# Modulation columns all on VectorE, two branches pulled forward, and the later modulation sums tied to stages of the delta rule

## The chip, the cores and the metric

The kernel runs on one core of one Trainium2 chip. The metric is the device time of one execution in microseconds (us). TensorE (PE) multiplies matrices, VectorE (DVE) does elementwise arithmetic and reductions, ScalarE (ACT) evaluates functions and copies, GpSimd (POOL) fills and issues a few transfers, and SyncE (SP) issues nearly all the transfers from HBM.

## The reference, cut to what the change touches

The model has a mixing block with four branches and a feed-forward part, and then two attention layers. Only the mixing block is touched. Its input has 512 tokens of 1024 features:

```
c_act = silu(c)
sh1, sc1, gt1, sh2, sc2, gt2 = split(c_act @ ada_w + ada_b, 6)     # 48 columns of 128 values
h = rms_norm(x, norm_mix_g) * (1 + sc1) + sh1
p = h @ w_in
y_a = rwkv7 delta rule (token shift, low-rank decays, two groups of two heads, chunks of 64)
y_b = gelu(p_u) * (causal w_s @ layer_norm(gelu(p_v)))             # gated branch
y_c = short convolution of width 3
y_d = s5: complex diagonal state space, then gelu and a gated product
x = x + gt1 * ((sum of sigmoid(gates) * y) @ w_o)
```

## The kernel before, in words

Every product is kept near full precision by splitting both operands into a high and a low part: a weight slab is loaded into `raw` (a ring of four buffers), ScalarE writes `whi`, VectorE writes `wlo` (three buffers each, lines 150 to 163), and `mm3` (line 178) makes three TensorE products for each pair of 128-row pieces. A slab of 128 output columns is thus 24 products of 512 columns.

The code is traced in program order, and a list scheduler then orders each engine's instructions by when it thinks that they are ready, earlier traced work first among what is ready. Buffers are asked for in the same way. `tc.issue_after(i)` adds an edge of order alone: what is traced in the block on the engine of `i` is queued behind `i`.

`_start` (line 374) makes the columns 8 to 15 of the modulation (sc1), two at a time. Six of them are dot products on VectorE (`tensor_tensor_reduce`, 1024 elements in each partition). Columns 8 and 15 (`BY_PE`) are made on TensorE from another layout of the weights, `ada_k`, and from the column form of c, `c_col`. Each pair of columns gives `g1` (line 444), which scales the x tiles (lines 448 to 455); the first three projection slabs run as the pairs come.

`_first_block` (line 1252) then runs the other four slabs of the delta rule's projection with the shift columns 0 to 7, small tables of the state space (`_s5_setup`), the convolution (`_conv_branch`, six slabs), and the gated branch (`_sg_branch`): four value products `svp` (96 matmuls), gelu and layer norm on VectorE, then two gate slabs and the small mixing matmuls `sgm`. `_merge(K, 2, ...)` sums the convolution with its gates: eight slabs, each of nine pieces (24 `gp` products, 6 `yp` products). At its piece 26 the large state space tables are traced (`_s5_tables`). After it come `_rwkv_shift` and all of `_s5_branch`: two projection slabs, transposes (`s5b`, `s5c`), input products `s5w`, a chain on VectorE with two scans that ends in the tiles `xb` (line 1216), then the output products `s5y` (line 1225) and more transposes.

Last come the two head groups of the delta rule, `_wkv`, a generator of 50 stages each. Stages 13 to 27 are five levels of three stages (`pu`, `pmt`, `pm`), 33 to 39 carry the state (`st`), and 40 to 47 make the output. Pieces of the merges 1 and 3 are poured between the stages as fill: 42 pieces first, then 1.3 for each stage. From stage 18 of either group every second stage also asks for one of the modulation columns 16 to 47: its weights go into the ring `raw`, and VectorE makes the dot product (`_dot`, line 333).

Of the kernel before, what the change touches and what calls it, by code (L numbers as in the profile page):

```python
# [17 lines left out]
AF = mybir.ActivationFunctionType  # L18
OP = mybir.AluOpType
# [25 lines left out]
VHEAD = 56  # L45


BY_PE = (8, 15)

A_ORDER = (6, 2, 0, 4, 3, 1, 5)  # L50

SHIFT_AT = 5
# [2 lines left out]

PIECES_FIRST, PIECES = 42, 1.3

ADA_FROM = 18


def _tri(n):
# [312 lines left out]
def _start(K):  # L374

    nc, V, d = K.nc, K.nc.vector, K.dram
    K.modv = K.const.tile([128, 48], F32, name="modv")  # L380
    K.c_row = K.g("c_row", "cr", shape=(128, D))
    c = K.g("c", "e4", shape=(128, D))
    cc = K.g("c_col", "rk")
    nc.scalar.dma_start(cc[:, 8:16], d["c_col"])
    for q in range(2):
        o = slice(q * 512, (q + 1) * 512)
        nc.sync.dma_start(c[:, o], d["c"][:, o])
    nc.sync.dma_start(K.vecs[:, 0:VHEAD], d["vecs"][:, 0:VHEAD])
    nc.scalar.activation(cc[:, 0:8], cc[:, 8:16], AF.Tanh, scale=0.5)
    V.scalar_tensor_tensor(cc[:, 0:8], cc[:, 0:8], 1.0, cc[:, 8:16], OP.add, OP.mult)  # L390
    for q in range(2):
        o = slice(q * 512, (q + 1) * 512)
        nc.scalar.activation(K.c_row[:, o], c[:, o], AF.Tanh, scale=0.5)
        V.scalar_tensor_tensor(K.c_row[:, o], K.c_row[:, o], 1.0, c[:, o], OP.add, OP.mult)
    g1 = K.const.tile([128, 8], F32, name="g1")
    x, K.h, w, ps = [], [], [], []

    def slab(after):
        raw, hi, lo = (K.wpool.tile([128, K.WMAX], t, name=n, tag=n, bufs=m)[:, 0:1024]
                       for n, t, m in (("raw", F32, 4), ("whi", F32R, 3), ("wlo", F32R, 3)))  # L400
        with K.tc.issue_after(after):
            nc.sync.dma_start(raw, d["w_in"][A_ORDER[len(w)]])
        w.append([t.rearrange("p (k c) -> p k c", k=8) for t in (hi, lo)])
        ps.append(K.mm())
        nc.scalar.activation(hi, raw, AF.Copy)
        return raw, hi, lo

    def lower(scaled, raw, hi, lo):
        with K.tc.issue_after(scaled):
            V.tensor_tensor(lo, raw, hi.bitcast(F32), OP.subtract)  # L410

    def products(i, k0, k1):

        T = nc.tensor
        for k in range(k0, k1):
            T.matmul(ps[i], lhsT=w[i][0][:, k], rhs=K.h[k][0], start=k == 0, stop=False)
            T.matmul(ps[i], lhsT=w[i][0][:, k], rhs=K.h[k][1], start=False, stop=False)
        for k in range(k0, k1):
            T.matmul(ps[i], lhsT=w[i][1][:, k], rhs=K.h[k][0], start=False, stop=k == KD - 1)

    done, new = [0, 0, 0], []
    for q in range(4):
        ks, on_pe = slice(2 * q, 2 * q + 2), None
        m = K.modv[:, 8 + 2 * q:10 + 2 * q]
        for j in range(8 + 2 * q, 10 + 2 * q):
            mj, b = K.modv[:, j:j + 1], K.vec("ada_b", j)
            if j in BY_PE:
                mp, aw = K.sm("ada_p")[:, 0:1], K.g("ada_k", "e4", shape=(128, 8, 128))
                nc.sync.dma_start(aw, d["ada_k"][BY_PE.index(j)].rearrange("p (k c) -> p k c", k=8))
                asked = nc.cur_bb.bb.instructions[-1]  # L430
                for k in range(8):
                    nc.tensor.matmul(mp, lhsT=aw[:, k], rhs=cc[:, k:k + 1], start=k == 0, stop=k == 7)
                on_pe = mj, mp, b
            else:
                aw = K.g("ada_w", "e4", shape=(128, 1024))
                nc.sync.dma_start(aw, d["ada_w"][j])
                asked = nc.cur_bb.bb.instructions[-1]
                V.tensor_tensor_reduce(aw, aw, K.c_row, 0.5, 0.0, OP.mult, OP.add, mj)
                V.tensor_tensor(mj, mj, b, OP.add)
                dot = nc.cur_bb.bb.instructions[-1]  # L440
        if on_pe is not None:
            with K.tc.issue_after(dot):
                V.scalar_tensor_tensor(on_pe[0], on_pe[1], 0.5, on_pe[2], OP.mult, OP.add)
        V.scalar_tensor_tensor(g1[:, ks], m, 1.0, K.vec("norm_mix_g", 2 * q, 2), OP.add, OP.mult)
        scaled = nc.cur_bb.bb.instructions[-1]
        if q == 0:
            new.append(slab(asked))
        for k in range(2 * q, 2 * q + 2):
            x.append(K.g(f"x{k}", "xr"))
            with K.tc.issue_after(asked):  # L450
                nc.sync.dma_start(x[k], d["x"][k])
            asked = nc.cur_bb.bb.instructions[-1]
            if k == 2 * q and q < 3:
                lower(scaled, *new[q])
            K.h.append(K.split(x[k], "h", g1[:, k:k + 1]))
        if q < 2:
            new.append(slab(asked))
        for i in range(min(q + 1, 3)):
            products(i, done[i], 2 * q + 2)
            done[i] = 2 * q + 2  # L460
    with K.tc.issue_after(asked):
        K.tables()
    K.loaded = asked
    K.split_1 = K.last
    acc = K.g("rms_a", "yd")
    for k in range(KD):
        sq = K.g("rms_q", "yd") if k else acc
        with K.tc.issue_after(K.hi_last):
            nc.scalar.activation(sq, x[k], AF.Square)
        if k:  # L470
            with K.tc.issue_after(K.split_1):
                V.tensor_tensor(acc, acc, sq, OP.add)
    return x, g1, acc, ps
# [491 lines left out]
def _sg_branch(K, after):  # L965
    nc, d = K.nc, K.dram
    with K.tc.tile_pool(name="sgp", bufs=1, side="right") as sp:
# [18 lines left out]
        for q in range(2):  # L986
            z = K.g("sgz", "xr")
# [13 lines left out]
            for b in range(2):  # L1001
# [2 lines left out]
                nc.vector.tensor_tensor(z3[:, b], z3[:, b], lnw[:, 1], OP.add)  # L1004
                vn.append(z3[:, b])
        K.sg_normed = nc.cur_bb.bb.instructions[-1]
        out = []
        for i in range(2):
            u = K.g("sgu", "xr")
# [10 lines left out]
            nc.vector.tensor_tensor(mx, mx, u, OP.mult)  # L1020
            K.tap(f"yb{i}", mx)
            out.append(K.split(mx, "y", 0.5))
    return out


def _cmul(V, ore, oim, are, aim, bre, bim, t, conj=False):
# [140 lines left out]
def _s5_branch(K, tab):  # L1167
# [44 lines left out]
    for x in range(2):  # L1212
        nc.gpsimd.memset(xb[x], 0.0)
        for h in range(2):
            hs = slice(h * 64, (h + 1) * 64)
            V.tensor_copy(xb[x][hs, :, h, 1:64], z[x][hs, :, 0:63])

    yb = K.g("s5_yb", "e4", shape=(128, 16, 64))
    for q in range(2):
# [19 lines left out]
    for i in range(2):  # L1239
# [6 lines left out]
        g2 = K.g("s5g", "e")  # L1246
        K.gelu2(g2, y, "e")
        out.append(K.split(g2, "yd", 0.5))
    return out


def _first_block(K):
    nc, d = K.nc, K.dram
    with ExitStack() as mix:
# [5 lines left out]
        with K.tags(e=9, e4=8):  # L1260
            with K.tc.tile_pool(name="s5", bufs=1) as sp:
                tiles, rs = _rwkv(K, *_start(K))
                last = K.last
                with K.tc.issue_after(last), K.tc.issue_after(K.loaded):
                    z = _s5_setup(K, sp)
                yc = _conv_branch(K)
                yb = _sg_branch(K, last)
                acc = [K.g(f"acc{m}", "xr") for m in range(8)]
                for n, _ in enumerate(_merge(K, 2, yc, acc)):
                    if n == 26:  # L1270
                        with K.tc.issue_after(K.sg_normed):
                            tab = _s5_tables(K, sp, z)
                la, pairs = _rwkv_shift(K, tiles, rs)
            yd = _s5_branch(K, tab)
        with K.tags(rw=16, rw4=4), K.tc.tile_pool(name="rwc", bufs=1) as cp:
            la = _wkv_consts(K, cp, la)
            ya, mg = [], []
            fill = chain(_merge(K, 1, yb, acc), _merge(K, 3, yd, acc))
            for _ in range(PIECES_FIRST):
                next(fill, None)  # L1280
            for i in range(2):
                for n, _ in enumerate(_wkv(K, i, la, pairs[i][1], pairs[i][0], pairs[i][2], ya)):
                    for _ in range(int((n + 1) * PIECES) - int(n * PIECES)):
                        next(fill, None)
                    if n >= ADA_FROM and n % 2 == 0:
                        next(ada, None)
        for _ in fill:
            pass
        for _ in ada:
# [397 lines left out]
def _slabs(w, kt, cols):  # L1687

    k, n = w.shape
    a = w.reshape(kt, 128, n // cols, cols).transpose(2, 1, 0, 3)  # L1690
    return np.ascontiguousarray(a).reshape(n // cols, 128, kt * cols)
# [9 lines left out]
def _columns(v):  # L1701

    return np.asarray(v).reshape(-1, 128).T


def _arrays(a):
# [2 lines left out]
    r["x"] = a["x"][0].T.reshape(8, 128, S)  # L1709
    r["c"] = np.broadcast_to(a["c"][0], (128, D))  # L1710
    r["mem"] = a["mem_2"][0].T.reshape(4, 2, 128, 256).transpose(0, 2, 1, 3).reshape(4, 128, 512)
    r["c_col"] = _columns(a["c"][0])
    r["ada_w"] = a["ada_w"][0].T.reshape(48, 128, 1024)
    r["ada_k"] = _slabs(np.concatenate([a["ada_w"][0][:, j * 128:(j + 1) * 128] for j in BY_PE], 1), 8, 128)
    r["w_in"] = _slabs(a["w_in"][0], 8, 128)
    r["w_in_t"] = a["w_in"][0][:, :896].T.reshape(7, 128, 1024)
    r["w_in_v"] = _halves(a["w_in"][0][:, 1152:1408], 256)[0]
# [46 lines left out]
```

## Time and profile before

| | us |
|---|---|
| median of 3 runs (lowest, highest) | 2145.5 (2145.1, 2149.9) |
| the profiled execution's own time | 2143.36 |
| its span in the trace | 2141.6 |
| TensorE busy in the span | 2090.3 |
| VectorE busy | 1416.4 |
| ScalarE busy | 934.8 |

Busy time of TensorE counts a matmul from its start to its modelled end, at whichever clock it runs, so a stretch at half clock is busy too. The granted clock (PEclk, a share of 2.4 GHz) tells the two apart. The median of the runs lies 2.1 us above the profiled execution's own time, and that 1.8 us above its span.

### The profile page before, as it was taken

The numbers are of one execution on the slowest core, as the hardware profiler recorded it, in microseconds if no ns is written. First come the engines' busy times: TensorE is split into PE (matmuls) and PEld (weight loads), VectorE is DVE, ScalarE is ACT, GpSimd is POOL, SyncE is SP. The second block draws the span as 40 slices with busy tenths as digits, with TensorE's granted clock in tenths as the row PEclk, the third lists the DMA queues.
The fourth block names the chain that finished last, engine by engine and source line by source line (L and its number), as shares of the span: only waits on it lengthen the run. The fifth ranks groups of instructions, "written<-read, shape, count | busy, mean of one in ns | idle before, by whom it ended". The sixth has DMA issues, their size and how long they took to land.

```text
span 2141.6 us, 29585 instructions
## 1 busy us (share of the span) xinstructions
PE 2090.3 (98%) x11534; PEld 1696.5 (79%) x11534; DVE 1416.4 (66%) x2667; ACT 934.8 (44%) x1551; POOL 21.9 (1%) x41
## 2 busy tenths in 40 slices
PE   7999999999999999999999999999999999999998
PEld 6878777778888888897778888888887778888887
DVE  7885886955744343567876756747668867575775
ACT  4433533323423232446764433424469954243433
POOL 0001000000000000000000000000000000000000
PEclk9989999999999999999999999999999999999999
DMA  8324353524332222242213222232321122323322
GB/s 319 113 73 146 102 167 106 192 70 138 108 99 98 89 99 99 90 129 80 82 58 97 90 99 96 92 99 81 128 72 48 60 79 83 105 84 103 99 77 71
DMA packets 68779, 220.47 MB, mean 103 GB/s; under 512 B 8500, under 2 KB 11604, under 8 KB 68640
## 3 DMA queue, kind: packets, MB, share of 16 engines
q1 hardware_dynamic: 65424, 210.72, 29.9%
q0 software_dynamic: 1920, 5.77, 0.9%
q8 instruction: 91, 1.49, 0.3%
q10 hardware_dynamic: 1296, 2.10, 0.3%
q14 instruction: 48, 0.39, 0.1%
HBM read 215.26 MB, written 3.30 MB: 102 GB/s over the span
## 4 chain that ended last, share of the span: by engine, by line
PE 87%; DVE 5%; ACT 4%; DMA 2%; issue 1%; SPq 0%; DVEq 0%; ACTq 0%
PE mm L183 64%; PE gp L183 7%; PE vt L183 3%; PE yp L183 2%; PE pT L1427 1%; PE po L1440 1%; PE fin L183 1%; PE s L1407 1%; DMA x<-x 1%; ACT whi L160 1%; PE s L1408 1%; ACT p L1415 1%; DVE wlo L161 1%; PE svp L183 1%; DVE raw L337 0%
## 5 line engine op out<-in xcount | busy, mean ns | idle before, releaser
L183 PE MATMUL mm<-hi,whi 128*128 128x512 f32 x2064 | 815.8, 396 | 3.0 <-ACT whi L160 1.6
L183 PE MATMUL mm<-hi,wlo 128*128 128x512 f32 x2064 | 816.5, 396 | 0.7 <-DVE wlo L161 0.7
L183 PE MATMUL mm<-lo,whi 128*128 128x512 f32 x2064 | 813.1, 394 | 0.6 <-DVE lo L1317 0.5
L160 ACT ACTIVATE whi<-raw 128x1024 fp32r<-128x1024 f32 (+3 forms) x338 | 347.3, 1030 | 741.1 <-PE mm L183 580.2
L161 DVE TENSOR_TENSOR wlo<-raw,whi 128x1024 fp32r<-128x1024 f32 (+3 forms) x338 | 399.9, 1186 | 171.9 <-ACT whi L160 155.3
L183 PEld LDWEIGHTS mm<-hi,whi 128*128 128x128 f32 x2064 | 389.4, 189 | 88.8 <-ACT hi L169 3.4
L183 PEld LDWEIGHTS mm<-lo,whi 128*128 128x128 f32 x2064 | 388.5, 188 | 87.4 <-DVE lo L1317 1.2
L183 PEld LDWEIGHTS mm<-hi,wlo 128*128 128x128 f32 x2064 | 388.3, 188 | 86.5 <-DVE wlo L161 1.3
L1612 DVE TENSOR_TENSOR u<-mm,spr 128x512 f32<-128x512 f32 x88 | 60.6, 688 | 80.6 <-PE mm L183 80.3
L183 PE MATMUL gp<-hi,whi 128*128 128x512 f32 x256 | 103.3, 404 | 3.6 <-ACT th L923 2.6
L183 PE MATMUL gp<-hi,wlo 128*128 128x512 f32 x256 | 102.8, 402 | 0.3 <-DVE wlo L161 0.3
L183 PE MATMUL gp<-lo,whi 128*128 128x512 f32 x256 | 102.3, 400 | 0.0
L1632 DVE TENSOR_TENSOR x<-x,mm 128x512 f32<-128x512 f32 x48 | 33.0, 687 | 94.9 <-PE mm L183 94.9
L1330 DVE SCALAR_TENSOR_TENSOR x<-mm,modv,x 128x512 f32<-128x512 f32 x32 | 24.0, 751 | 90.3 <-PE mm L183 90.3
L1613 ACT ACTIVATE cv<-u,vecs 128x512 f32<-128x512 f32 x88 | 71.2, 810 | 2.9 <-DVE u L1612 2.9
L1615 DVE SCALAR_TENSOR_TENSOR cv<-u,vecs,cv 128x510 f32<-128x510 f32 x88 | 66.0, 750 | 3.1
L1614 DVE SCALAR_TENSOR_TENSOR cv<-u,vecs,cv 128x511 f32<-128x511 f32 x88 | 65.7, 746 | 2.1 <-ACT cv L1613 1.8
L1623 ACT ACTIVATE cth<-cv 128x512 f32<-128x512 f32 x44 | 27.8, 632 | 86.5 <-DVE cv L1615 86.5
L183 PEld LDWEIGHTS gp<-hi,whi 128*128 128x128 f32 x256 | 48.6, 190 | 16.1 <-ACT th L923 3.5
L1415 ACT ACTIVATE p<-p,at_m 128x128 f32<-128x128 f32 (+1 forms) x96 | 53.4, 557 | 14.8 <-DVE at_m L1414 13.8
L183 PEld LDWEIGHTS gp<-hi,wlo 128*128 128x128 f32 x256 | 48.5, 189 | 11.9 <-DVE wlo L161 1.0
L1427 PE MATMUL pT<-k_ident,p 128*128 128x128 f32 x304 | 53.9, 280 | 2.9 <-ACT p L1424 2.4
(549 smaller groups left out, 2671.4 us busy)
## 6 DMA issues: line engine op xcount, KB each, us to landing
raw<-w_up SPq DMA_DIRECT2D x88, 512.0 KB, 3.3
raw<-ffn_w SPq DMA_DIRECT2D x64, 512.0 KB, 3.3
raw<-w_in SPq DMA_DIRECT2D x49, 512.0 KB, 3.5
raw<-ada_w SPq DMA_DIRECT2D x32, 512.0 KB, 4.2
raw<-w_down SPq DMA_DIRECT2D x32, 384.0 KB, 3.1
raw<-w_out SPq DMA_DIRECT2D x16, 512.0 KB, 3.3
raw<-w_down SPq DMA_DIRECT2D x16, 512.0 KB, 3.2
ada_w<-ada_w SPq DMA_DIRECT2D x14, 512.0 KB, 9.2
```

What stands on the lines that cost most here:

```text
L160: nc.scalar.activation(hi[:, :n], raw[:, :n], AF.Copy)
L161: nc.vector.tensor_tensor(lo[:, :n], raw[:, :n], hi[:, :n].bitcast(F32), OP.subtract)
L183: self.nc.tensor.matmul(out, lhsT=a, rhs=b, start=first and n == 0, stop=last and n == total - 1)
L1330: V.scalar_tensor_tensor(K.xr[m], ps, K.modv[:, 40 + m:41 + m], K.xr[m], OP.mult, OP.add)
L1415: A.activation(p[:, 0:n], p[:, 0:n], AF.Exp, bias=nm, scale=-1.0, accum_out=l)
L1427: T.transpose(pp[:, b * 128:(b + 1) * 128], p[:, b * 128:(b + 1) * 128], K.ident)
L1612: V.tensor_tensor(u, ps, rs, OP.mult)
L1613: A.activation(c, u, AF.Identity, bias=K.vec("conv_b_2", l * 44 + j), scale=tap(2))
L1614: V.scalar_tensor_tensor(c[:, 1:], u[:, 0:S - 1], tap(1), c[:, 1:], OP.mult, OP.add)
L1615: V.scalar_tensor_tensor(c[:, 2:], u[:, 0:S - 2], tap(0), c[:, 2:], OP.mult, OP.add)
L1623: A.activation(th, gt, AF.Tanh, scale=0.5)
L1632: V.tensor_tensor(K.xr[m], K.xr[m], ps, OP.add)
```

## The change

All eight scale columns are made on VectorE, and the two layouts for TensorE, with their silu in column form, are gone. The bias is added to both columns of a pair at once. The load of the head of the vector table is issued behind the first two columns' loads. The gated branch becomes a generator: its value products and its norm are traced ahead of the convolution, the rest behind it. The state space branch becomes one too: its projection, transposes, input products and the chain up to `xb` are traced at piece 44 of the first merge, the rest where it was. The dot products of the columns 16 to 47 are asked for from stage 12 of the first head group and from stage 24 of the second, and each is queued behind the last VectorE instruction that was traced before it.

```diff
-BY_PE = (8, 15)
-ADA_FROM = 18
+ADA_FROM = (12, 24)
@@ _start
-    cc = K.g("c_col", "rk")
-    nc.scalar.dma_start(cc[:, 8:16], d["c_col"])
...
-    nc.sync.dma_start(K.vecs[:, 0:VHEAD], d["vecs"][:, 0:VHEAD])
-    nc.scalar.activation(cc[:, 0:8], cc[:, 8:16], AF.Tanh, scale=0.5)
-    V.scalar_tensor_tensor(cc[:, 0:8], cc[:, 0:8], 1.0, cc[:, 8:16], OP.add, OP.mult)
...
         for j in range(8 + 2 * q, 10 + 2 * q):
-            mj, b = K.modv[:, j:j + 1], K.vec("ada_b", j)
-            if j in BY_PE:
-                ... eight matmuls into ada_p
-            else:
-                ... dot product, then the add of one bias
+            aw = K.g("ada_w", "e4", shape=(128, 1024))
+            nc.sync.dma_start(aw, d["ada_w"][j])
+            asked = nc.cur_bb.bb.instructions[-1]
+            V.tensor_tensor_reduce(aw, aw, K.c_row, 0.5, 0.0, OP.mult, OP.add, K.modv[:, j:j + 1])
+        if q == 0:
+            with K.tc.issue_after(asked):
+                nc.sync.dma_start(K.vecs[:, 0:VHEAD], d["vecs"][:, 0:VHEAD])
                 asked = nc.cur_bb.bb.instructions[-1]
-        if on_pe is not None:
-            with K.tc.issue_after(dot):
-                V.scalar_tensor_tensor(on_pe[0], on_pe[1], 0.5, on_pe[2], OP.mult, OP.add)
+        V.tensor_tensor(m, m, K.vec("ada_b", 8 + 2 * q, 2), OP.add)
@@ _sg_branch
         K.sg_normed = nc.cur_bb.bb.instructions[-1]
+        yield
...
-    return out
+    yield out
@@ _s5_branch
             V.tensor_copy(xb[x][hs, :, h, 1:64], z[x][hs, :, 0:63])
+    yield
...
-    return out
+    yield out
@@ _first_block
+                sg = _sg_branch(K, last)
+                next(sg)
                 yc = _conv_branch(K)
-                yb = _sg_branch(K, last)
+                yb = next(sg)
+                next(sg, None)
...
                     if n == 26:
                         with K.tc.issue_after(K.sg_normed):
-                            tab = _s5_tables(K, sp, z)
+                            s5 = _s5_branch(K, _s5_tables(K, sp, z))
+                    if n == 44:
+                        next(s5)
                 la, pairs = _rwkv_shift(K, tiles, rs)
-            yd = _s5_branch(K, tab)
+            yd = next(s5)
...
-                    if n >= ADA_FROM and n % 2 == 0:
-                        next(ada, None)
+                    if n >= ADA_FROM[i] and n % 2 == 0:
+                        dve = [v for v in nc.cur_bb.bb.instructions[-60:] if v.engine == K.last.engine]
+                        with K.tc.issue_after(dve[-1]):
+                            next(ada, None)
```

## Rows read from the trace of the kernel before

**Rows 1.** The page's first part: busy time, share of the span, instructions.

```profile
PE 2090.3 (98%) x11534; PEld 1696.5 (79%) x11534; DVE 1416.4 (66%) x2667; ACT 934.8 (44%) x1551; POOL 21.9 (1%) x41
```

**Rows 2.** Timeline, TensorE: start, duration, instruction, then idle time before it and releaser.

```profile
114.59 0.69 PE L1015 MATMUL sgm<-sg_wsT,sgz 128*64 128x128 f32 x4 [2.54 <-ACT gl_s L258]
...
232.13 0.50 PE L183 MATMUL gp<-hi,whi 128*128 128x512 f32 x1 [2.29 <-ACT th L923]
...
233.41 0.89 PE L1225 MATMUL s5y<-s_xb,s_W 128*128 128x128 f32 x4 [0.55 <-DVE s_xb L1216]
...
412.01 1.15 PE L723 MATMUL pmt<-MT,u 64*64 64x64 f32 x32 [0.69 <-ACT u L718]
...
416.55 1.15 PE L717 MATMUL pu<-M,bk 64*64 64x64 f32 x32 [2.46 <-DVE bk L713]
418.69 0.58 PE L723 MATMUL pmt<-MT,u 64*64 64x64 f32 x6 [0.99 <-ACT u L718]
```

**Rows 3.** Windows of 10 us: length, each engine's busy time (instructions), PEclk, DMA share, GB/s.

```profile
110.00:120.00 10.00, 7.46 (x26) 4.99 (x26) 9.65 (x43) 3.08 (x5) 0.00 (x0) 0.71 0.30 106
120.00:130.00 10.00, 9.91 (x58) 7.80 (x58) 7.21 (x12) 2.66 (x4) 0.00 (x0) 0.94 0.16 52
...
150.00:160.00 10.00, 10.00 (x43) 8.56 (x43) 7.15 (x25) 1.43 (x2) 2.77 (x6) 0.66 0.40 129
...
200.00:210.00 10.00, 9.94 (x105) 7.87 (x106) 4.55 (x11) 5.44 (x21) 1.17 (x2) 1.00 0.69 227
...
230.00:240.00 10.00, 7.32 (x33) 6.66 (x34) 9.86 (x17) 5.29 (x9) 0.00 (x0) 0.69 0.01 2
```

**Rows 4.** Windows of 20 us in the second head group, same columns.

```profile
400.00:420.00 20.00, 15.87 (x278) 13.27 (x278) 20.00 (x36) 4.88 (x7) 0.00 (x0) 0.95 0.59 190
420.00:440.00 20.00, 20.00 (x320) 16.65 (x318) 8.55 (x13) 5.55 (x9) 0.00 (x0) 0.96 0.43 148
```

**Rows 5.** Timeline of the start, TensorE, VectorE and ScalarE.

```profile
7.77 3.55 PE L432 MATMUL ada_p<-c_col,ada_k 128*128 128x1 f32 x16 [7.77 <-DMA ada_k<-ada_k]
9.20 1.23 DVE L438 CUSTOM_DVE_ANT_0 ada_w<-ada_w,c_row 128x1024 f32<-128x1024 f32 x1 [3.31 <-DMA ada_w<-ada_w]
...
11.35 0.16 DVE L443 SCALAR_TENSOR_TENSOR modv<-ada_p,vecs 128x1 f32<-128x1 f32 x1 [0.72 <-PE ada_p L432]
...
11.74 1.34 ACT L169 ACTIVATE hi<-x,g 128x512 fp32r<-128x512 f32 x2 [0.31 <-DVE g L444]
...
25.96 1.84 PE L432 MATMUL ada_p<-c_col,ada_k 128*128 128x1 f32 x16
...
37.73 0.50 PE L183 MATMUL mm<-hi,wlo 128*128 128x512 f32 x1 [0.70 <-DVE wlo L161]
```

**Rows 6.** Windows of 40 and 60 us, columns as in the third group.

```profile
60.00:120.00 60.00, 57.46 (x288) 47.27 (x287) 52.82 (x195) 23.69 (x38) 0.00 (x0) 0.95 0.34 113
...
260.00:300.00 40.00, 39.19 (x269) 31.05 (x270) 38.18 (x80) 21.07 (x39) 0.55 (x1) 1.00 0.45 148
...
360.00:420.00 60.00, 54.83 (x551) 44.58 (x553) 57.79 (x118) 23.41 (x44) 0.00 (x0) 0.98 0.55 177
```

**Rows 7.** Chain that ended last, from 100 to 270 us: one slab of the first merge.

```profile
133.04 5.54 PE gp L183 x24
138.57 1.39 PE yp L183 x6
```

**Rows 8.** The state space chain on VectorE: its first product (timeline), its last copies (tile s_xb).

```profile
212.07 0.69 DVE L1029 TENSOR_TENSOR s_z<-s_b,s_ph 128x512 f32<-128x512 f32 x1
...
L1216 DVE COPY s_xb<-s_z x4: 404/418/420, 231.2 to 233.7; 64x504 f32<-64x504 f32 x4
```

**Rows 9.** Tile raw, 240 to 470 us: loads and dots; min/median/max ns, first and last start.

```profile
L335 SPq DMA_DIRECT2D raw<-ada_w x32: 327/328/516, 254.8 to 411.1; - x32
L337 DVE CUSTOM_DVE_ANT_0 raw<-raw,c_row x32: 1215/1219/1226, 258.7 to 418.1; 128x1024 f32<-128x1024 f32 x32
```

**Rows 10.** Window of the tile gp alone: length, TensorE (gate products), loads, ScalarE, clock.

```profile
200.00:266.00 66.00, 34.86 (x138) 25.33 (x138) 2.90 (x5) 0.95 0.38 126
```

More of the change, by code (lines that the diff above doesn't have):

```diff
@@ L422, in _start @@
     for q in range(4):
-        ks, on_pe = slice(2 * q, 2 * q + 2), None
+        ks = slice(2 * q, 2 * q + 2)
         m = K.modv[:, 8 + 2 * q:10 + 2 * q]
         for j in range(8 + 2 * q, 10 + 2 * q):
-            mj, b = K.modv[:, j:j + 1], K.vec("ada_b", j)
-            if j in BY_PE:
-                mp, aw = K.sm("ada_p")[:, 0:1], K.g("ada_k", "e4", shape=(128, 8, 128))
-                nc.sync.dma_start(aw, d["ada_k"][BY_PE.index(j)].rearrange("p (k c) -> p k c", k=8))
-                asked = nc.cur_bb.bb.instructions[-1]
-                for k in range(8):
-                    nc.tensor.matmul(mp, lhsT=aw[:, k], rhs=cc[:, k:k + 1], start=k == 0, stop=k == 7)
-                on_pe = mj, mp, b
-            else:
[L435 to L440, printed above, removed]
-        if on_pe is not None:
-            with K.tc.issue_after(dot):
-                V.scalar_tensor_tensor(on_pe[0], on_pe[1], 0.5, on_pe[2], OP.mult, OP.add)
+            aw = K.g("ada_w", "e4", shape=(128, 1024))
[5 more added lines that the diff above has]
+                nc.sync.dma_start(K.vecs[:, 0:VHEAD], d["vecs"][:, 0:VHEAD])
+                asked = nc.cur_bb.bb.instructions[-1]
+        V.tensor_tensor(m, m, K.vec("ada_b", 8 + 2 * q, 2), OP.add)
         V.scalar_tensor_tensor(g1[:, ks], m, 1.0, K.vec("norm_mix_g", 2 * q, 2), OP.add, OP.mult)
@@ L1711, in _arrays @@
     r["mem"] = a["mem_2"][0].T.reshape(4, 2, 128, 256).transpose(0, 2, 1, 3).reshape(4, 128, 512)
-    r["c_col"] = _columns(a["c"][0])
     r["ada_w"] = a["ada_w"][0].T.reshape(48, 128, 1024)
-    r["ada_k"] = _slabs(np.concatenate([a["ada_w"][0][:, j * 128:(j + 1) * 128] for j in BY_PE], 1), 8, 128)
     r["w_in"] = _slabs(a["w_in"][0], 8, 128)
```

## The prediction

> **What bounds the kernel now.** I read the page's first part, then the waits of TensorE, then its clock by windows, then what VectorE did where TensorE waited. TensorE is busy for 98% of the span, 51 us short of all of it [rows 1], so nothing that is taken off another engine pays by itself. Two things pay: a wait of TensorE that goes, and a stretch at half clock that goes with it. The second is hidden in the busy share: at 120 to 130 us TensorE is busy for 9.91 of 10 us, yet its clock is 0.94, and 0.71 in the 10 us before [rows 3].
>
> The edits touch four places of TensorE's own timeline. First, the start, where the first projection product waits for scale columns and the sixteen little products of `ada_p` run twice [rows 5]. Second, 114.59: TensorE stands 2.54 us before `sgm`. The line names an early gelu as releaser, but that was long done; the missing operand is the normed tile, which VectorE makes until then. Third, 232.13 and 233.41: 2.29 and 0.55 us before `s5y`, until `xb` is there. Fourth, 412 to 419: 0.69, 2.46 and 0.99 us inside the levels of the second head group [rows 2], while VectorE is busy for 20.00 of 20 us [rows 4].
>
> What a fallen clock costs: the time at 1.2 GHz does half the work, so one minus the mean clock, times the window. At the second place that is 0.29 of 10 and 0.06 of 10 us, 3.5 us, of which I put about 0.4 into the wait itself: 3.1. At the third it is 0.31 of 10: 3.1 us [rows 3]. At the fourth 0.05 and 0.04 of 20 us, 1.8, less 0.4 in the last wait: 1.4 [rows 4].
>
> **The start.** Columns 8 and 9 are now two dots of 1.23 us. The row shows the dot of column 9 at 9.20, when its weights land; column 8 takes the place of `ada_k`, which had landed by 7.77, so its dot is over before 9.20. After 9.20 come 1.23, a read of the sum, one bias add and `g` of 0.16 each: about 10.8. Before, the same `g` waited until 11.35 for TensorE's column, and ScalarE stood 0.31 us for it ahead of `hi` at 11.74 [rows 5]. ScalarE had the slab's high part to make until 11.43, so of the 0.7 us only 0.3 arrives: -0.3. The silu of the column form and its load, on ScalarE's queue, go; they hindered nobody. On SP's queue the order is c, two column loads, vector table, slab, x: the table moves behind two loads and the slab keeps its place. The table is wanted at about 10.4, with `raw` and x behind it, and the column that is waited for is ahead of it; if it were late, ScalarE's wait would grow one for one, up to the 0.7 just won.
>
> Column 15 costs VectorE another 1.23 us at about 26, while it was waiting for TensorE anyway; TensorE loses sixteen products of 1.84 us in all [rows 5]. That is not all gain: at 37.73 it stood for a `wlo` from VectorE [rows 5], whose work before that point hardly changes. Between none and all of the 1.84 I take 0.5, since the row nearest to the end of the stretch is a wait for VectorE. Together -0.8; at best 0.3 and 1.84, -2.1. On the bad side the longer idle before 37.73 may pull the clock down, as the wait at 114.59 did, for 3.1: +2.8 at worst, when only the 0.3 is won.
>
> **The gated branch ahead of the convolution.** No instruction is added; its two value slabs move ahead of six convolution slabs in SP's queue and in `raw`, with its small table loads, as before. Six slabs of 5.5 us [rows 7] now lie between the value products and `sgm`, far more than the norm needs. The wait and its clock go: 2.54 and 3.1, -5.6. What is behind the norm on VectorE now: the `wlo` of the convolution's slabs. From 60 to 120 us VectorE is busy for 52.82 us [rows 6]; the same work must now fit into about 54. The cover is thin: the three prefetched slabs. If it fails, waits for `wlo` can give back the whole 5.6. Nearest is the row itself, in which the small state space setup, the shift and the splits were interleaved at 88% and no wait is listed; I take 1.0 of new waits. Sum -4.6, between -5.6 and 0.
>
> **The state space inputs in the first merge.** Moved: two slab loads and their splits, 48 products, transposes, `s5w`, two fills on POOL, and the chain on VectorE. That chain took from 212.07 to about 234 [rows 8], about 22 us, with other work in between. Traced at piece 44 of 72, it has three slabs of 5.54 and 1.39 us [rows 7] to run beside, 21 us, and the shift's small matmuls; and its first products no longer share VectorE with the shift's dots. So `s5y` should find `xb` ready: -2.84 and -3.1, -5.9. The shift itself is now traced behind some 17 us more of TensorE work; the slack is the 42 fill pieces and the rest of the state space branch, which TensorE does first. If the shift is late all the same, fill runs on further ahead and nothing stops; I take 0, and 2 us if that cover fails too.
>
> A rule that speaks against this move: the transposes `s5b` and `s5c`. From 200 to 210 us they run in the old order with a few gate products between them, and the clock is 1.00 [rows 3]; in the new order there are gate products of the first merge to put between them, so I count 0. The Trainium skill, "TensorE: Matmul & The Clock Gate", section "Part 4: PE-mode transpose", says that transposes do not count as TensorE being busy for its clock in the way that products do. By the row the sum stays; by the rule there may be one more fall of the clock, like the one at 150 to 160 us after small table products, 0.34 of 10, 3.4 us [rows 3].
>
> **The later sums.** There were 32 dots of 1.22 us, spread from 258.7 to 418.1 [rows 9]: as soon as their weights lay in `raw`, in front of the delta rule's own short steps. VectorE was busy 38.18 of 40 us from 260 to 300 and 57.79 of 60 from 360 to 420 [rows 6]. Now none is asked for in stages 0 to 11 of the first group or 0 to 23 of the second, the two full stretches. So the fourth place's 4.14 and 1.4 go: -5.5.
>
> The cost is in `raw`. A dot that waits for its stage keeps its buffer until then, and there are four. Buffers are asked for in program order: the first gate slab of merge 3 is piece 72, traced at stage 23, behind the sums of stages 16 to 22 and two slabs of `s5_glu_w`. With four buffers it can be loaded when the sum of stage 20 is done, and is split about a level later. So fill cannot run ahead of program order there. In the old run it had done 138/24 = 5.75 gate slabs at 266 us [rows 10], where program order asks for 42/9 = 4.67: it was a slab ahead, 6.9 us [rows 7]. That slab is missing in levels two to five of the first group. A level without fill showed 0.69 or 0.99, and 2.46 us of idle [rows 2]; of the latter pair, 3.45, up to one dot of 1.22 is the dots' own doing: 2.2 to 3.45, say 2.9. Two such levels: +5.8. Bounds: 0, if the chain is so quick without dots that fill never gets ahead; and for the worst, three levels there (8.7) and two in the second group, whose fill ends in program order at stage 28, before the first slab of merge 0 can get a buffer (5.8), and a fall of the clock at each (3.1 each): 20.7. Sum of this part +0.3, between -5.5 and +15.2.
>
> **Sum.** -0.8 - 4.6 - 5.9 + 0.3 = -11.0. From 2143.36, the profiled execution's own time, that is 2132.4; the median of the runs shown lies 2.1 us above it, so 2134 us.
>
> **The rivals.** *The waits move on* (same): VectorE is the bound from 70 to 200. The whole 5.6 of the gated branch is given back as waits for `wlo`, and the tables, behind them, make `xb` late by half of its 5.9. For it: 52.82 of 60; against it: no wait of TensorE in that stretch before [rows 6]. -11.0 + 4.6 + 2.95 = -3.5: 2142 us. That the second move does not do what it says is the second half of this.
>
> *The ring starves half the fill* (same): four unfilled levels instead of two, +5.8: -5.2, 2140 us. For it: the ring's order; against: a stage that is not crowded by dots needs less fill.
>
> *The ring starves TensorE* (slower): one mechanism, at the fill of both head groups. At its bound, 20.7 instead of 5.8, the sum is +3.9 (2149); with a second pair of unfilled levels behind stage 28, 2 x 2.9 + 3.1, it is +12.8 (2158). It decides the sign from 16.8 us of new idle there, and passes 0.3% at 23.2. Against it: in the light last stages fill comes first in program order and takes its time.
>
> *The clock falls at the moved transposes* (faster): +3.4, 2138 us. That is the rule of "Part 4: PE-mode transpose" in the Trainium skill's page on TensorE; the row at 200 to 210 us bears it out for the old order only in that it did not happen there.
>
> **How the numbers follow.** My forecast 0.58, the transposes 0.12, the moving waits 0.10, the half-starved ring 0.11, the starved ring 0.09. A change within 0.3% (6.4 us) is about what a measurement of this kernel can't tell from none: faster is below 2139, slower above 2152. So faster 0.70, same 0.21, slower 0.09. The low end is the good bounds together, -2.1 - 5.6 - 5.9 - 5.5 = -19.1, and half of the 3.4 us at 150 to 160, should the new order break up those small products: 2125. The high end takes in the moving waits and the half-starved ring and leaves the starved one out: 2145.
>
> **What would show it.** Right: no idle over 0.5 us before `sgm` and `s5y`, a clock of 1.00 around them, `g` of the first pair before 11, no dot before stage 12, and VectorE below 90% in the second group's first half. Wrong: waits for `wlo` or `whi` between 70 and 120; gate products waiting for `whi` in the first group's levels, with their slab's load issued behind a dot; PEclk below 1 at the moved transposes or before 37. The prediction falls if the delta rule's stretch, from its first small matmul to the first product of `w_o`, gets longer by over 5 us.

## The result, and the profile after

| | before | after |
|---|---|---|
| median of 4 runs (us) | 2147.16 | 2180.06 |
| lowest, highest | 2145.1, 2149.9 | 2178.86, 2183.65 |
| profiled execution, its span | 2143.36, 2141.6 | 2183.65, 2181.8 |

The change makes the kernel slower: 1.0166 of before, with an interval of 1.0148 to 1.0185; the medians of this table alone give 1.0153. The kernel before has one run more here than when the forecast, 2134, was made.

The page's first part, after [rows 1]: TensorE is busy for 18 us more, and idle for 22 us more.

```profile
PE 2108.5 (97%) x11502; PEld 1706.1 (78%) x11502; DVE 1416.4 (65%) x2666; ACT 934.8 (43%) x1550; POOL 21.8 (1%) x41
```

Timeline of TensorE, the places where it stands still up to the first head group [rows 2, 5]:

```profile
11.71 0.79 PE L408 MATMUL mm<-hi,whi 128*128 128x512 f32 x1 [11.71 <-ACT hi L167]
...
35.73 0.79 PE L181 MATMUL mm<-hi,whi 128*128 128x512 f32 x1 [2.62 <-ACT whi L158]
...
64.46 0.38 PE L181 MATMUL svp<-whi,hi 128*128 128x256 f32 x1 [1.40 <-ACT rp L837]
65.17 0.39 PE L181 MATMUL svp<-wlo,hi 128*128 128x256 f32 x1 [0.32 <-DVE wlo L159]
...
248.93 0.50 PE L181 MATMUL gp<-hi,whi 128*128 128x512 f32 x1 [3.41 <-ACT whi L158]
```

The waits before `sgm` and `s5y` are gone, and others stand elsewhere: one behind the start, one at the value products `svp`, which now come while ScalarE and VectorE still make the h tiles (1.40 us until ScalarE's copy `rp`, then 0.32 us until `wlo`), and one of a gate product. The windows of 10 us (columns as in [rows 3]) show the clock that went with them:

```profile
30.00:40.00 10.00, 7.38 (x24) 5.36 (x23) 8.73 (x11) 7.19 (x12) 0.00 (x0) 0.76 1.01 404
...
60.00:70.00 10.00, 8.28 (x44) 7.37 (x43) 10.00 (x14) 7.33 (x10) 0.00 (x0) 0.83 0.16 54
...
110.00:120.00 10.00, 10.00 (x55) 7.91 (x55) 10.00 (x12) 3.73 (x5) 0.00 (x0) 1.00 0.29 101
...
180.00:190.00 10.00, 10.00 (x110) 8.01 (x109) 4.77 (x8) 4.88 (x17) 1.90 (x2) 1.00 0.17 54
...
230.00:240.00 10.00, 10.00 (x44) 8.09 (x43) 8.30 (x22) 4.93 (x8) 0.55 (x1) 1.00 0.42 143
...
250.00:260.00 10.00, 10.00 (x38) 8.02 (x37) 6.96 (x12) 7.89 (x14) 0.00 (x0) 0.83 0.32 105
```

At the first head group the kernel is still some 3 us ahead, by the number of products done. Then come the two head groups. Timeline of TensorE, three levels of the first group and the second half of the second one:

```profile
292.59 1.15 PE L700 MATMUL pu<-M,bk 64*64 64x64 f32 x32 [3.07 <-DVE bk L696]
...
300.09 1.15 PE L700 MATMUL pu<-M,bk 64*64 64x64 f32 x32 [2.08 <-DVE bk L696]
...
308.51 1.97 PE L700 MATMUL pu<-M,bk 64*64 64x64 f32 x32 [3.23 <-DVE modv L348]
...
439.41 1.97 PE L700 MATMUL pu<-M,bk 64*64 64x64 f32 x32 [4.34 <-DVE modv L348]
...
462.66 0.50 PE L577 MATMUL om<-hi,blkr 128*128 128x512 f32 x1 [1.35 <-ACT hi L167]
466.40 0.79 PE L577 MATMUL om<-lo,blkr 128*128 128x512 f32 x1 [3.24 <-DVE lo L170]
470.20 1.87 PE L546 MATMUL hr_c<-k_blk,sq 128*128 128x2 f32 x8 [3.01 <-ACT sq L783]
```

No gate product lies between these levels: TensorE has nothing to do while VectorE makes `bk`. (`modv` in two lines is a bias add that stands on VectorE behind `bk`; what was waited for is `bk`.) With the 0.7 us before each `pmt`, and waits of the state steps, the idle time is 10.5 us in the first group and 16.0 in the second. Windows of 40 us at these two times, before and then after (not quite the same work: the mean over heads `om` of the second group comes at 449.6 us before and at 462.7 after):

```profile
280.00:320.00 40.00, 38.93 (x504) 31.46 (x503) 34.58 (x66) 12.37 (x25) 0.00 (x0) 1.00 0.58 191
440.00:480.00 40.00, 37.36 (x333) 29.41 (x330) 22.23 (x46) 10.81 (x17) 0.00 (x0) 1.00 0.25 76
```

```profile
280.00:320.00 40.00, 29.55 (x460) 26.37 (x459) 24.58 (x42) 11.58 (x23) 0.00 (x0) 0.83 0.30 100
440.00:480.00 40.00, 28.99 (x375) 24.90 (x373) 22.86 (x55) 7.16 (x10) 0.00 (x0) 0.73 0.55 185
```

By the clock 0.17 and 0.27 of 40 us are lost, 6.8 and 10.8 us, part of it inside the idle time. Why fill is missing stands on SP's queue (timeline of SP; a line that groups several loads spans the time from the first to the last):

```profile
264.97 27.22 SPq L333 DMA_DIRECT2D raw<-ada_w  x4
293.61 7.82 SPq L157 DMA_DIRECT2D raw<-s_glu_w  x2
307.79 0.33 SPq L157 DMA_DIRECT2D raw<-w_in  x1
...
435.19 27.23 SPq L333 DMA_DIRECT2D raw<-ada_w  x9
463.44 0.33 SPq L157 DMA_DIRECT2D raw<-rwkv_out  x1
464.58 1.51 SPq L157 DMA_DIRECT2D raw<-w_in  x2
```

Four loads for sums take 27 us, because each needs a buffer that a tied dot still holds; the first gate slab of merge 3 goes out at 307.79. VectorE's timeline there shows what let it go, the dot that ends at 307.7:

```profile
305.94 0.68 DVE L717 TENSOR_TENSOR MT<-pmt,MT 128x512 f32<-128x512 f32 x1
306.54 1.22 DVE L335 CUSTOM_DVE_ANT_0 raw<-raw,c_row 128x1024 f32<-128x1024 f32 x1
307.68 0.08 DVE L335 DVE_READ_ACCUMULATOR2_ANT modv<- 128x1 f32 x1
307.68 0.69 DVE L696 TENSOR_TENSOR bk<-at,k_masks 128x512 f32<-128x512 f32 x1
```

The dot also stands in front of `bk`. In the second group nine loads for sums hold the queue from 435 to 462, and merge 0's first slab follows at 464.58. In the kernel before, that slab was asked for at 414.63, and its products began at 421.95, between the small ones (timelines of SP and TensorE before):

```profile
414.63 6.16 SPq L159 DMA_DIRECT2D raw<-w_in  x4
...
421.95 0.50 PE L183 MATMUL gp<-hi,whi 128*128 128x512 f32 x1
```

### The profile page after: what moved, and what is told of

Read it like the earlier page. It is cut to its first block, busy times and chain, and to the rows that moved or that the text cites. A ratio compares the mean times of both kernels' runs of the same rounds, so it can differ in the third digit from the quotient of the medians.

```text
span 2181.8 us, 29526 instructions
## 1 busy us (share of the span) xinstructions
PE 2108.5 (97%) x11502; PEld 1706.1 (78%) x11502; DVE 1416.4 (65%) x2666; ACT 934.8 (43%) x1550; POOL 21.8 (1%) x41
## 4 chain that ended last, share of the span: by engine, by line
PE 87%; DVE 5%; ACT 4%; DMA 2%; issue 1%; SPq 0%; DVEq 0%; ACTq 0%
PE mm L181 63%; PE gp L181 8%; PE vt L181 3%; PE yp L181 2%; PE pT L1419 1%; PE po L1432 1%; PE fin L181 1%; PE s L1399 1%; DMA w_t<-w_in_t 1%; ACT whi L158 1%; PE s L1400 1%; DMA ada_w<-ada_w 1%; PE pmt L706 1%; PE svp L181 1%; ACT p L1407 1%
## 5 line engine op out<-in xcount | busy, mean ns | idle before, releaser
L181 PEld LDWEIGHTS gp<-lo,whi 128*128 128x128 f32 x256 | 49.2, 192 | 10.8 <-issue 0.8
```

What stands on the lines that cost most here:

```text
L181: self.nc.tensor.matmul(out, lhsT=a, rhs=b, start=first and n == 0, stop=last and n == total - 1)
```

## The experiments

Ratios are to the kernel before on the same chip (its median 2143.9 to 2144.4 there), with their 95% intervals.

**The later sums alone, and everything but them.** Edit of `before_new_sums`: the last part of the diff on the kernel before. Edit of `after_old_sums`:

```diff
-ADA_FROM = (12, 24)
+ADA_FROM = 18
-                    if n >= ADA_FROM[i] and n % 2 == 0:
-                        dve = ...
-                        with K.tc.issue_after(dve[-1]):
-                            next(ada, None)
+                    if n >= ADA_FROM and n % 2 == 0:
+                        next(ada, None)
```

> The kernel before with the later sums alone changed (stages 12 and 24, tied). Both theories: 33 to 38 us slower than before, 2180 to 2185. Rival, that the sums only hurt because the other parts had changed what fill has done by then: 2165 or less.

> The changed kernel with the later sums as before (from stage 18 of both groups, not tied); the other three parts stay. Theory 1, the held ring: tied dots keep the buffers of raw, and the gate slabs queue behind them on SP, which cost some 33 us between the first small matmul of the delta rule and the first product of w_o; without it the lead of about 5 us that the changed kernel has at the first head group stays: 2142 us (2138 to 2147). Theory 2, the dots in the chain on VectorE, expects the same. Rival: the start and the moved branches are the loss: above 2155.

Measured: the sums alone 2176.73, 1.0156 (1.0132 to 1.0179); without them 2147.93, 1.0016 (1.0004 to 1.0027). The sums make all of the loss but some 3 us, much as foretold from the trace (the first run lies 3 us under its range, the second 1 us above its own). Nothing of the gain of the other three parts arrives: that is a second question, below.

**The stage or the tie.** Edit of `after_untied`: `next(ada, None)` without the `issue_after`, the stages stay.

> The changed kernel, sums asked for from stages 12 and 24, but not tied to VectorE's order: a dot runs as soon as its weights lie there. Theory 1 (a buffer held until the stage): buffers come free at once, 2140 to 2150. Theory 2 (dots between the delta rule's steps, wherever the buffers are): dots still stand in that chain as they did before the change: 2145 to 2160. Rival, that the late stage is the loss because merge 0's slabs are asked for behind the last sums: 2165 or more.

Measured: 2144.91, 1.0007 (0.9994 to 1.0019). The tie costs some 34 us and the stages nothing; by the medians they are 3 us better than the old ones.

**Which group.** Edit of both: the tie `if i == 0` or `if i == 1`.

> The changed kernel with the sums tied in the first head group alone; those of the second run when their weights are there. By the traces of the changed kernel and the untied one the first group (from its start to its mean over heads, with the same gate products done) loses about 16 us: 2161 us (2157 to 2165). If the held buffers of the first group also delay the second: 2168 or more. If only the second group loses: 2145 to 2148.

> The changed kernel with the sums tied in the second head group alone. By the same traces this group loses about 19 us, since the first slabs of merge 0 stand on SP's queue behind the sums of its stages 24 to 48: 2164 us (2158 to 2168). Rival, as the prediction had it: fill reaches merge 0 after two unfilled levels, 3 to 9 us: 2148 to 2154.

Measured: 2162.64, 1.0086 (1.0067 to 1.0105), and 2160.80, 1.0080 (1.0066 to 1.0094): by the ratios 17 and 16 us above the untied kernel, each loss where its ties are. Windows of 40 us of the first of the two kernels, then of the second:

```profile
280.00:320.00 40.00, 29.55 (x480) 26.25 (x480) 23.64 (x41) 10.66 (x21) 0.00 (x0) 0.79 0.33 106
420.00:460.00 40.00, 36.47 (x668) 30.19 (x667) 20.77 (x38) 9.54 (x14) 0.00 (x0) 0.96 0.34 113
```

```profile
280.00:320.00 40.00, 39.31 (x574) 32.19 (x575) 36.62 (x66) 13.32 (x27) 0.00 (x0) 1.00 0.60 199
420.00:460.00 40.00, 29.40 (x351) 25.44 (x352) 22.91 (x54) 6.82 (x10) 0.00 (x0) 0.68 0.51 176
```

The idle time and the low clock (the last but two column) change places with the tie.

**Held buffers, or dots in the chain.** Edit of `after_no_loads` (the weights of columns 16 to 47 are left out):

```diff
-            raw = K.wpool.tile(...)
...
-        _dot(K, raw, K.dram["ada_w"][j], K.c_row, K.modv[:, j:j + 1], 0.5, after)
+            K.nc.vector.tensor_tensor_reduce(K.c_row, K.c_row, K.c_row, 0.0, 0.0, OP.mult, OP.add, K.modv[:, j:j + 1])
```

> The changed kernel with all ties, but the later sums read only what lies on the chip (the row of c with itself, times zero): the weights of columns 16 to 47 are left out, and with them 32 loads and all use of raw for sums. The dots stand in the same places of the delta rule's chain on VectorE. Theory 1 (held buffers and the gate slabs queued behind them): fill flows, 2140 to 2150. Theory 2 (dots in front of the delta rule's steps): the loss stays, 2168 or more.

Edit of `after_own_ring`: the sums' weights in a tile `ada_raw` with one buffer, loaded by `K.nc.gpsimd.dma_start`; `raw` with `bufs=3`.

> The changed kernel with its stages and ties, but the weights of the later sums have a buffer of their own (one, taken from raw, which keeps three) and are asked for on POOL's queue. Theory 1: gate slabs are no longer behind held buffers, fill runs on in both groups: 2140 to 2155. Theory 2: the dots stand in the same places of VectorE's order, so the loss stays: 2170 or more.

Measured: without the loads 2150.70, 1.0027 (1.0017 to 1.0037), just above what the held buffers expected. So the dots' place in the chain costs some 4 to 6 us, and the loads and their buffers the other 28 to 30. The own buffer gave 2163.71, 1.0094 (1.0071 to 1.0117), between the two theories. Its first head group is cured: from `z` to `om`, with the same gate products done, 93.3 us (258.57 to 351.86), against 107.7 with the ties and 91.7 without. What it loses later looks like its own doing, by the trace's summary of its tile: with one buffer a dot comes every 5 to 8 us only, and dots of the first group run into the crowded start of the second. A ring of its own with more buffers was not run, so this is read from the trace and not shown by a run.

```profile
L335 POOL DMA_DIRECT2D ada_raw<-ada_w x32: 527/527/675, 131.8 to 503.7; - x32
...
  DMA ada_raw<-ada_w: 28.1, 16
```

(VectorE sat idle 28.1 us, 16 times, until such a load was there.)

**The other parts, one by one**, each on the kernel before, its edit the part of the diff under `_start`, under `_sg_branch`, under `_s5_branch`, and the last two together.

> The kernel before with the start alone changed (all eight scale columns on VectorE, the table behind two loads). By the trace of the changed kernel: the first product 0.8 us earlier, then one wait of about 2.6 us before the fourth slab, half the clock behind it, and the stage of the norm's sum 1 to 2.3 us later: 2145.5 to 2147, 0.05 to 0.1% slower than before. Rival, the prediction's own: 0.8 us faster. A second question: in the changed kernel and in the two with its start and its branches, the products of the feed-forward follow each other every 0.2320 us, in the kernel before and the one with the new sums alone every 0.2305, which makes some 9 us from the feed-forward to the end. If the start brings that: 2154 to 2157.

> The kernel before with the gated branch alone moved ahead of the convolution. The prediction said -4.6 with 1.0 of new waits; the trace of the changed kernel shows 3.8 us lost at the value products (a wait and the clock): -1.8 by these two, or -3.3 to -4.6 by the way from the norm's sum to the first table product in that trace: 2140 to 2142.5. Rival, waits for wlo give it all back: 2144 to 2145. If this move brings the 0.2320 us spacing of the feed-forward's products: 2149 to 2152.

> The kernel before with the state space inputs alone moved into the first merge. The prediction said -5.9; the trace of the changed kernel has no wait before s5y but a new one of 3.4 us, of a gate product for whi at 248.9, so about -3: 2141 (2139 to 2143). Rival, the new wait and its clock give it all back: 2144 to 2146. If this move brings the 0.2320 us spacing: 2150 to 2154.

> Both moved branches on the kernel before, with its start and its later sums. If the two add up and the spacing of the feed-forward's products stays 0.2305 us: 2136 to 2139. If the slower spacing of 0.2320 comes with either: 2146 to 2149.

Measured: the start 2142.46, 1.0000 (0.9991 to 1.0009); the gated branch 2153.97, 1.0047 (1.0033 to 1.0061); the state space 2143.94, 0.9996 (0.9987 to 1.0005); both branches 2152.01, 1.0035 (1.0022 to 1.0047). None gains, and none lies in its expected range: the start is 3 us under it, nearer to the prediction's own rival, the state space 1 us above, and the two with the gated branch 2 to 3 us above what they would take with the slower spacing. Timeline of TensorE in the kernel with the gated branch alone:

```profile
62.92 0.38 PE L183 MATMUL svp<-whi,hi 128*128 128x256 f32 x1 [0.58 <-ACT rp L854]
67.17 0.58 PE L183 MATMUL svp<-wlo,hi 128*128 128x256 f32 x1 [3.87 <-DVE wlo L161]
...
231.32 1.19 PE L1226 MATMUL s5y<-s_xb,s_W 128*128 128x128 f32 x4 [3.35 <-DVE s_xb L1217]
```

The 2.54 us before `sgm` came back as 4.5 us at `svp`. Before `s5y` TensorE stands for 3.35 us where it stood for 2.29 and 0.55, but it comes there earlier: `s5y` starts at 231.32 instead of 233.41. And something else is there. Windows of 240 us in the feed-forward, far behind all that was changed: before, then with the gated branch alone.

```profile
640.00:880.00 240.00, 240.00 (x1044) 195.71 (x1043) 100.17 (x115) 75.28 (x97) 0.00 (x0) 1.00 0.29 96
```

```profile
640.00:880.00 240.00, 240.00 (x1036) 194.45 (x1035) 97.63 (x110) 72.73 (x93) 0.00 (x0) 1.00 0.28 95
```

TensorE never stands and its clock is 1.00 in both, but 1036 products fit where 1044 did. From the first sum of a norm in the feed-forward to the end the one took 1596.2 us (545.44 to 2141.6), the other 1605.2 (546.04 to 2151.2): 9 us. All 12 kernels with the gated branch ahead have the slower spacing, and the five without it that keep the rings' places have the faster one.

**Where the weight rings lie.** Edit of `before_gap`, `after_untied_gap` and `after_gap`, which moves tiles and nothing else:

```diff
-    K.modv = K.const.tile([128, 48], F32, name="modv")
+    first = [K.wpool.tile([128, K.WMAX], F32R, name="whi", tag="whi", bufs=3)]
+    K.modv = K.wpool.tile([128, 48], F32, name="modv", tag="modv", bufs=1)
...
+        hi = (first.pop() if first else K.wpool.tile(..., tag="whi", bufs=3))[:, 0:1024]
```

> The kernel before with the same change of place of the two rings. Theory A: here it hurts, since the two slabs in three with unequally numbered buffers are now an odd multiple of 64 bytes apart: spacing 0.2312 to 0.2315 instead of 0.2305, 2148 to 2151. Rival B: no change, 2143 to 2146. Rival C, the new place is better or worse whatever the pairs: as many us and of the same sign as in the changed kernel.

> The changed kernel, sums untied, and the rings of whi and wlo placed otherwise: nothing is computed or ordered differently, the first buffer of wlo lies 29312 bytes behind that of whi instead of 12480. Theory A: the slower spacing of the products behind the gated branch's move comes from which buffers of whi and wlo a slab gets. In all kernels with the move a slab has equally numbered buffers, 12480 bytes apart, and 0.2320 us from product to product; in the others two slabs in three have the second of one and the third of the other, 16640 or 8320 bytes apart (both even multiples of 64, where 12480 is an odd one), and their trace shows about 0.229 in those and 0.2325 in the third. With 29312, an even multiple, every slab has about 0.229: 15 to 20 us less than the 2144.9 without it, 2124 to 2131. Rival B: the numbers of the buffers or something else of the move: spacing and time stay, 2143 to 2147.

> The changed kernel with ties, and the rings of whi and wlo placed as in the two others. Theory A: 15 to 20 us off its 2180: 2160 to 2165, with the whole of the loss at the head groups left. Rival B: 2178 to 2183.

Measured: 2150.43, 1.0027 (1.0018 to 1.0036); 2146.10, 1.0001 (0.9992 to 1.0011); 2181.68, 1.0157 (1.0141 to 1.0173). The kernel before lost 6 us, as theory A said, by places alone: TensorE ran the same 11534 products in the same order. Its window:

```profile
640.00:880.00 240.00, 240.00 (x1037) 194.43 (x1036) 100.04 (x116) 75.00 (x97) 0.00 (x0) 1.00 0.29 95
```

But the kernels with the branch ahead did not gain the 15 to 20 us. What theory A started from holds about: in the kernel before, the spacing goes round in threes, as the rings do with their three buffers. First products of four slabs on end (timeline of TensorE), before, then with the gated branch alone:

```profile
641.23 0.39 PE L183 MATMUL mm<-hi,whi 128*128 128x512 f32 x1
...
646.73 0.39 PE L183 MATMUL mm<-hi,whi 128*128 128x512 f32 x1
...
652.30 0.40 PE L183 MATMUL mm<-hi,whi 128*128 128x512 f32 x1
...
657.82 0.39 PE L183 MATMUL mm<-hi,whi 128*128 128x512 f32 x1
```

```profile
642.20 0.40 PE L183 MATMUL mm<-hi,whi 128*128 128x512 f32 x1
...
647.76 0.40 PE L183 MATMUL mm<-hi,whi 128*128 128x512 f32 x1
...
653.38 0.39 PE L183 MATMUL mm<-hi,whi 128*128 128x512 f32 x1
...
658.90 0.40 PE L183 MATMUL mm<-hi,whi 128*128 128x512 f32 x1
```

A slab of 24 products takes 5.50, 5.57 and 5.52 us in turn before, and 5.56, 5.62 and 5.52 with the branch ahead. Over the whole window that is 229.2, 232.2 and 230.1 ns a product, and 231.9, 233.9 and 230.4. So the slabs of the kernels with the branch ahead are not alike, though theory A gives them one distance; and in `after_untied_gap`, where it gives every slab the good distance, they take 232.9, 231.6 and 231.1. Theory A's rule has fallen; that places matter has not. One more trial, the rings in the order `whi`, `wlo`, `raw`:

> The changed kernel with untied sums, and the rings in another order (whi, wlo, raw instead of raw, whi, wlo): the same distance of 12480 bytes between the two buffers of a slab, each 16640 bytes further to the front. What is open: whether the 0.2320 us spacing hangs on the distance within a pair of equally numbered buffers (then it stays, 2143 to 2147), or on where the buffers lie (then it can go to 0.2305, 2134 to 2138). That the place matters in some way is shown by the kernel before, which went from 0.2305 to 0.2320 when only places changed.

Measured: 2147.66, 1.0014 (1.0005 to 1.0023), and the slower spacing stayed, with the same three values to 0.1 ns: moving both rings together changes nothing here. Which places or distances are good stays open, and so does whether the gated branch's move gets its slower spacing by them; that is likely, not shown.

**What is left without the two losses.** `start_states_untied` is the diff without its part under `_sg_branch` and without the tie.

> What is left of the change without its two losses: the start, the state space inputs in the first merge, the sums from stages 12 and 24 without ties; the gated branch stays behind the convolution. Alone the start measured 1.0 and the state space move 0.9996 of before, and dropping the ties as well as the old stages took 3 us off. Theory (the slower spacing comes with the gated branch's move alone): spacing 0.2305 us in the feed-forward and 2140 to 2143. Rival, the parts fill the same slack and do not add up, or the slower spacing comes here too: 2144 to 2152.

Measured: 2138.04, 0.9970 (0.9959 to 0.9980), by the medians some 6 us faster than before and 42 faster than after, and 2 us under the range of its theory. Its `sgm` still waits 2.54 us; the faster spacing stays. Page part 1 and the window:

```profile
PE 2082.7 (97%) x11502; PEld 1688.1 (79%) x11502; DVE 1417.7 (66%) x2666; ACT 934.3 (44%) x1550; POOL 22.0 (1%) x41
```

```profile
640.00:880.00 240.00, 240.00 (x1043) 195.73 (x1042) 101.63 (x119) 76.72 (x101) 0.00 (x0) 1.00 0.28 96
```

## Why the prediction was wrong

Of the 46 us between forecast and result, some 32 are the later sums (forecast +0.3, alone +32 by the medians) and some 14 the other three parts (forecast -11.3, together +3.5).

**The start** (-0.8). The first product came 0.8 us earlier, and so it did in the mean of the traces (12.0 us in the twelve kernels with this start, 12.7 in the six without it); 0.3 had been worked out for it. Alone the part measured no change within 2 us. The longer idle time that it named came too, 2.62 us instead of 1.20 and 0.70, and so did the clock fall in this execution: 0.76 and 0.90 in two windows of 10 us, 3.4 us, where the bad side had 3.1.

**The gated branch ahead** (-4.6). The wait before `sgm` and its clock went. The step that failed is "I take 1.0 of new waits". It looked for late `wlo` among the convolution's slabs; the wait came earlier, at the value products themselves, while VectorE is at 10.00 of 10 us with the h tiles. In the kernel after it is 1.40 us for ScalarE's `rp` and 0.32 for `wlo`, with a clock of 0.83 in those 10 us (1.7 us); with the move alone it is 0.58 and 3.87. That is the first half of the rival of the moving waits. Its second half, a late `xb`, did not come: with the move alone `s5y` starts 2.1 us earlier. And the 9 us of slower spacing were in no step.

**The state space inputs** (-5.9). The waits before `s5y` and the clock of 0.69 went, and s5's transposes, now at 178 to 183 us, left the clock at 1.00. The fall that the rule of the Trainium skill ("TensorE: Matmul & The Clock Gate", "Part 4: PE-mode transpose") allowed did not come. But a gate product now waits 3.4 us for `whi` at 248.9, with a clock of 0.83 in the 10 us behind it (1.7 us): on ScalarE that slab stands behind the `rkv` of the shift, which waits for VectorE. The step that failed is the shift, "I take 0, and 2 us if that cover fails too"; alone the part measured -2.8 to +1.1 us.

**The later sums** (+0.3, bounds -5.5 to +15.2). The prediction had the mechanism, the order in `raw`, and named what would show it: a gate slab's load issued behind a dot. It took two unfilled levels; the part measured +32 alone. Three steps failed. First, the bound for the second group, "before the first slab of merge 0 can get a buffer", let fill come back behind two levels. In the program's order merge 0 stands behind all sums, up to stage 48, and SP issues in that order: no fill from 431 to 470 us. The argument against the starved ring, that "in the light last stages fill comes first in program order", holds for merges 1 and 3 only, which were used up. Second, a level without fill cost 2.8 to 5.0 us instead of 2.9, since a tied dot can stand in front of `bk`. Third, a fall of the clock was priced at 3.1, as for a single wait; here the two windows of 40 us lost 6.8 and 10.8 us by the clock, part of it inside the idle time. So the rival "The ring starves TensorE", at 0.09, was the right one. Its time of 2149 to 2158 was too small: it has the sums at +15.2 to +24.1, for these three reasons, and the other three parts at -11.3.

## What to carry to other kernels

Before an operation is tied to a late stage, write down the buffer that it will hold and every load behind it on the issuing queue, up to the last tied one, not the first. Here leaving out the tie gave back all of its cost, and a ring and a queue of its own for the load cured the first group; a tie on the load as well was not run. Where fill was missing the clock fell too (0.83 and 0.73 in windows of 40 us that had 1.00 before), so price a lost filler by the idle time and by the clock. And look at the rate of a stretch that the change doesn't touch; if it moved, part of the difference has another cause than the one argued.

## What was not expected of the hardware

The spacing of equal products changed with where tiles lie in the on-chip memory: by places alone 1037 products instead of 1044 fit into 240 us at a clock of 1.00, 0.7% fewer, and from slab to slab it goes round in threes. No wait, clock or engine time of the profile shows it.

The clock can stay low while TensorE is busy. In the kernel after, behind the wait of 4.34 us, it was 0.50 for 10 us in which TensorE was busy for 8.64; a little later, with the small products `st` and `o` alone and 4.07 of 5 us busy, it was 1.00. What decides between the two no run here shows.

```profile
440.00:450.00 10.00, 8.64 (x124) 8.26 (x123) 1.17 (x3) 1.75 (x3) 0.00 (x0) 0.50 0.31 107
...
455.00:460.00 5.00, 4.07 (x114) 3.58 (x113) 3.96 (x11) 0.00 (x0) 0.00 (x0) 1.00 0.72 228
```

The same wait of 2.62 us behind the start went with a clock of 0.76 from 30 to 40 us in the profile after and of 1.00 in that of `start_states_untied`, so a single profile tells little about one fall. The Trainium skill ("TensorE: Matmul & The Clock Gate", "What's actually happening") says that the times at which the gate looks are not tied to the kernel's start; these two rows fit that and do not prove it.
